# Seven block products in the last down projection: 28 of its 44 input tiles, between the up tiles that follow

## The chip, the cores and the metric

The kernel runs on one core of one Trainium2 chip. The metric is device time in microseconds (us), from the start to the end of one execution, lower is better; the median of several executions is compared. Five engines work side by side, each through its own instruction queue in order: PE (TensorE, matrix products), DVE (VectorE) and ACT (ScalarE) for elementwise work, POOL, and SP, which here only starts the transfers of weights from HBM. A matrix product on PE multiplies a stationary 128x128 operand with a moving operand of up to 512 columns and adds the result to a bank of PSUM.

## The reference

Two encoder layers over 272 tokens (16 learned ones and 256 of the input), 2048 wide, in float32. What matters here is the second half of each layer, the feed-forward part:

```python
h2 = _rmsnorm(h_stream, norm_ffn[i])
up = h2 @ w_up[i]                                     # 2048 -> 2 x 5632
u_gate = _dwconv3_centred(up[..., :D_FF], w_conv[i], b_conv[i])
u_val = up[..., D_FF:]
h_stream = h_stream + (jax.nn.silu(u_gate) * u_val) @ w_down[i]   # 5632 -> 2048
```

The first half of a layer (projections, attention, a Fourier branch, gates, output projection) is not touched. After the last layer the 16 learned tokens are dropped, so the last down projection is needed for 256 tokens only.

## The kernel before

Activations lie transposed, channels on the 128 partitions and tokens along the free dimension; 128 channels are a tile. The down projection has 44 input tiles and 16 output tiles.

**Precision.** A float32 product is made of three cheaper ones: each operand is split into a high part (rounded to the type fp32r) and a low part (the rest), and high x high, high x low and low x high are added in PSUM. Weights are the stationary operand, activations the moving one.

**Weight chunks.** All weights come as one long list of chunks (`chunks`, L152) of 128 partitions x 1024 float32, 512 KB each: four input tiles by two output tiles. SP loads a chunk into one of 4 buffers `raw` (L161), ACT rounds it into `wh` (L202), DVE subtracts into `wl` (L205). `wh` and `wl` have 3 buffers each. So the cast of chunk i+3 cannot begin before PE has finished with chunk i, and the load of chunk i+4 not before DVE has finished with chunk i.

**Groups.** `group` (L229) takes the chunks of one pair of output tiles and issues their matmuls. Where 2 x 256 columns fit a bank (the last layer, L923), high and low activations lie side by side and one matmul of 512 columns (L253) does high x high and high x low, and one of 256 (L254) does low x high; otherwise there are three (L257 to L259). After every second step of the group, `step` runs a piece of the work in `shadow` (generators pushed by other stages) and `pump` a pending split.

**Feed-forward.** For a pass of input tiles (`FF_SPLIT`, 24 and then 20 tiles), a loop over pairs of tiles runs the gate half of the up projection (group `ug`, four chunks, 258 or 272 columns) and the value half (`uv`, four chunks). DVE and ACT make the convolution, the silu and the product in between (L946 to L967) and leave its high and low part in `gHL`. Then eight groups `d` of the down projection go over all tiles of the pass, and DVE adds each to the residual stream `XT` (L976, L982) or, in the last pass of the last layer, to `ot`, which ACT's queue sends out (L979, L980).

**Order.** The Python code emits the instructions of each engine, and a scheduler behind it may move an instruction within its engine's queue where its operands allow it. The order that comes out is fixed in the program.

Of the kernel before, what the change touches and what calls it, by code (L numbers as in the profile page):

```python
# [10 lines left out]
F32 = mybir.dt.float32  # L11
# [23 lines left out]
FF_SPLIT = (24, 20)  # L35
# [10 lines left out]
)  # L46
HC = 64
# [69 lines left out]
def encoder_kernel(ctx, tc, xT, params, consts, bmat, w_in, w_abr, w_four, w_f64, w_out, w_up, w_down, outT):  # L117
    nc = tc.nc
    per = ctx.enter_context(tc.tile_pool(name="per", bufs=1))
# [6 lines left out]
    for l in range(DEPTH):  # L126
        def g(w, mg, k0, k1):
            return [(w[l, mg, c], CW) for c in range(k0 // CW, k1 // CW)]
# [16 lines left out]
        for c, n in enumerate(FF_SPLIT):  # L145
            for i in range(k0 // MG, (k0 + n) // MG):
                order.append(((l, "ug", i), g(w_up, i, 0, KT)))
                order.append(((l, "uv", i), g(w_up, FT // MG + i, 0, KT)))
            for mg in range(8):
                order.append(((l, "d", c, mg), g(w_down, mg, k0, k0 + n)))  # L150
# [3 lines left out]
    wl_at = [WL_AT.get(k[:2], 0) for k, chs in order for _ in chs]  # L154
# [54 lines left out]
    shadow = []  # L209

    def push(gen, wait=0):
        shadow.append([wait, gen])

    def step(force=False):
        for s in shadow:
            s[0] -= 1
        for s in list(shadow):
            if force or s[0] <= 0:
                try:
                    s[0] = next(s[1])  # L220
                except StopIteration:
                    shadow.remove(s)
                return

    def drain():
        while shadow:
            step(True)

    def group(key, rhs, width, tag="mm"):  # L229
# [5 lines left out]
        nk = CW * len(chs)  # L235
        for j in range(len(chs)):
# [4 lines left out]
            st["next"] += 1  # L241
            cm = [(c, m) for c in range(CW) for m in range(MG)]
            if j == len(chs) - 1:
                cm.sort(key=lambda v: v[1])
# [227 lines left out]
    for l in range(DEPTH):  # L472
# [447 lines left out]
        with tc.tile_pool(name=f"ffn{l}", bufs=1) as fp:  # L920
            hold = {}
            push(norm_stats(hold), 8)
            fused = 2 * W2 <= 512  # L923
# [10 lines left out]
            for c, n in enumerate(FF_SPLIT):  # L934
                gHL = fp.tile([P, FF_SPLIT[0], 2, XP], F32R, tag="gHL", name="gHL")
                gH, gL = (gHL[:, :, e, G_AT[l][e]:G_AT[l][e] + T] for e in range(2))
                for i in range(k0 // MG, (k0 + n) // MG):
                    ps = group((l, "ug", i), xr(lo), W)
                    drain()
# [16 lines left out]
                    for m in range(MG):  # L956
                        j = 2 * i + m - k0
                        cv = cs[m]
                        val = ps[m][:, :W2]
                        if fused:  # L960
                            v = fp.tile([P, W2], F32, tag="v", name="v", bufs=2)
                            nc.scalar.copy(v, ps[m][:, W2:2 * W2])
                            nc.vector.tensor_tensor(v, v, val, op=ALU.add)
                            val = v
                        nc.vector.tensor_tensor(cv[:, lo2:T], cv[:, lo2:T], val, op=ALU.mult)
                        nc.scalar.copy(gH[:, j, lo2:T], cv[:, lo2:T])
                        nc.vector.tensor_tensor(gL[:, j, lo2:T], cv[:, lo2:T], gH[:, j, lo2:T].bitcast(F32), op=ALU.subtract)  # L967
                lastc = c == len(FF_SPLIT) - 1
                for mg in range(8):
                    two = fused and not (lastc and mg == 7)  # L970
                    ps = group((l, "d", c, mg), (lambda kt: (both(gHL, kt, G_AT[l]),)) if two
                               else (lambda kt: (gH[:, kt, lo2:T], gL[:, kt, lo2:T])), W2)
# [12 lines left out]
                k0 += n  # L985
# [51 lines left out]
```

## Time and profile before

| | before |
|---|---|
| median of 3 runs | 2530.57 us (2529.23 to 2531.3) |
| profiled execution | 2531.57 us |
| span of its instructions | 2529.6 us |
| PE busy | 2519.5 us, granted clock at full speed throughout |
| DVE busy / ACT busy | 1688.4 us / 1210.1 us |
| read from HBM / written | 457.35 MB / 2.10 MB |

"Busy" is the time in which an engine had at least one instruction under way; matmuls overlap one another, so their single durations add up to more than the time they take, and the price of one matmul is read from the distance between two starts. The feed-forward part of layer 0 begins at about 524 us and that of the last layer at about 1797.5 us. The last one has four stages: 12 pairs of up groups to 2064, the first down pass to 2194.5, 10 pairs of up groups to 2417, the second down pass to the end.

### The profile page before, as it was taken

The numbers are of one execution on the slowest core, as the hardware profiler recorded it, in microseconds if no ns is written. First come the engines' busy times: TensorE is split into PE (matmuls) and PEld (weight loads), VectorE is DVE, ScalarE is ACT, GpSimd is POOL, SyncE is SP. The second block draws the span as 40 slices with busy tenths as digits, with TensorE's granted clock in tenths as the row PEclk, the third lists the DMA queues.
The fourth block names the chain that finished last, engine by engine and source line by source line (L and its number), as shares of the span: only waits on it lengthen the run. The fifth ranks groups of instructions, "written<-read, shape, count | busy, mean of one in ns | idle before, by whom it ended". The sixth has DMA issues, their size and how long they took to land.

```text
span 2529.6 us, 47876 instructions
## 1 busy us (share of the span) xinstructions
PE 2519.5 (100%) x19740; PEld 2461.2 (97%) x19740; DVE 1688.4 (67%) x2691; ACT 1210.1 (48%) x1741; POOL 18.3 (1%) x37
## 2 busy tenths in 40 slices
PE   9999999999999999999999999999999999999999
PEld 9999999999999999999999999999999998999988
DVE  7687866766665446566566877677766665566654
ACT  6455544554444334444444554445545543454543
POOL 0000000000000000000000000000000000000000
PEclk9999999999999999999999999999999999999999
DMA  6444555555555555555554545555555555555564
GB/s 239 164 158 160 195 184 190 189 177 181 179 182 178 181 180 179 182 178 180 180 174 153 178 159 195 197 198 194 189 191 189 189 190 194 195 187 191 191 204 163
DMA packets 132155, 465.34 MB, mean 184 GB/s; under 512 B 15328, under 2 KB 19296, under 8 KB 131936
## 3 DMA queue, kind: packets, MB, share of 16 engines
q1 hardware_dynamic: 127568, 457.37, 53.2%
q10 hardware_dynamic: 4368, 4.92, 0.6%
q8 instruction: 154, 2.52, 0.4%
q14 instruction: 65, 0.53, 0.1%
HBM read 457.35 MB, written 2.10 MB: 182 GB/s over the span
## 4 chain that ended last, share of the span: by engine, by line
PE 96%; DVE 2%; ACT 1%; DMA 1%; issue 0%; ACTq 0%; SPq 0%; DVEq 0%
PE ps_ug L257 7%; PE ps_ug L259 7%; PE ps_ug L258 7%; PE ps_uv L253 6%; PE ps_d L253 6%; PE ps_d L259 4%; PE ps_d L257 4%; PE ps_d L258 4%; PE ps_uv L259 3%; PE ps_uv L257 3%; PE ps_uv L258 3%; PE ps_uv L254 3%; PE ps_d L254 3%; PE ps_o L257 2%; PE ps_o L259 2%; PE ps_o L258 2%
## 5 line engine op out<-in xcount | busy, mean ns | idle before, releaser
L205 DVE TENSOR_TENSOR wl<-raw,wh 128x1024 fp32r<-128x1024 f32 (+1 forms) x835 | 1016.8, 1220 | 672.8 <-ACT wh L202 669.4
L202 ACT CAST wh<-raw 128x1024 fp32r<-128x1024 f32 (+1 forms) x834 | 870.3, 1046 | 960.5 <-PE ps_ug L258 159.4
L257 PE MATMUL ps_ug<-xHL,wh 128*128 128x272 f32 (+1 forms) x1408 | 398.0, 283 | 0.0
L259 PE MATMUL ps_ug<-xHL,wl 128*128 128x272 f32 (+1 forms) x1408 | 396.5, 282 | 0.0
L258 PE MATMUL ps_ug<-xHL,wh 128*128 128x272 f32 (+1 forms) x1408 | 395.7, 281 | 0.0
L257 PEld LDWEIGHTS ps_ug<-xHL,wh 128*128 128x128 f32 x1408 | 264.3, 188 | 0.9
L258 PEld LDWEIGHTS ps_ug<-xHL,wh 128*128 128x128 f32 x1408 | 264.5, 188 | 0.1
L259 PEld LDWEIGHTS ps_ug<-xHL,wl 128*128 128x128 f32 x1408 | 264.3, 188 | 0.0
L253 PE MATMUL ps_uv<-xHL,wh 128*128 128x512 f32 x704 | 245.1, 391 | 0.0
L253 PE MATMUL ps_d<-gHL,wh 128*128 128x512 f32 x664 | 225.9, 389 | 0.0
L257 PE MATMUL ps_d<-gHL,wh 128*128 128x272 f32 (+1 forms) x744 | 212.5, 286 | 0.0
L259 PE MATMUL ps_d<-gHL,wl 128*128 128x272 f32 (+1 forms) x744 | 211.9, 285 | 0.0
L258 PE MATMUL ps_d<-gHL,wh 128*128 128x272 f32 (+1 forms) x744 | 211.2, 284 | 0.0
L257 PE MATMUL ps_uv<-xHL,wh 128*128 128x272 f32 x704 | 201.3, 286 | 0.0
L259 PE MATMUL ps_uv<-xHL,wl 128*128 128x272 f32 x704 | 200.6, 285 | 0.0
L258 PE MATMUL ps_uv<-xHL,wh 128*128 128x272 f32 x704 | 199.9, 284 | 0.0
L254 PE MATMUL ps_uv<-xHL,wl 128*128 128x256 f32 x704 | 198.4, 282 | 0.0
L254 PE MATMUL ps_d<-gHL,wl 128*128 128x256 f32 x664 | 183.3, 276 | 0.0
L253 PEld LDWEIGHTS ps_uv<-xHL,wh 128*128 128x128 f32 x704 | 131.9, 187 | 27.2
L253 PEld LDWEIGHTS ps_d<-gHL,wh 128*128 128x128 f32 x664 | 124.6, 188 | 25.5
L257 PE MATMUL ps_ga<-xHL,wh 128*128 128x272 f32 (+1 forms) x512 | 147.0, 287 | 0.1
L257 PE MATMUL ps_gf<-xHL,wh 128*128 128x272 f32 (+1 forms) x512 | 145.9, 285 | 0.1
(286 smaller groups left out, 5862.1 us busy)
## 6 DMA issues: line engine op xcount, KB each, us to landing
raw<-in_w_up SPq DMA_DIRECT2D x352, 512.0 KB, 3.5
raw<-in_w_in SPq DMA_DIRECT2D x206, 512.0 KB, 3.6
raw<-in_w_down SPq DMA_DIRECT2D x176, 512.0 KB, 3.5
raw<-in_w_out SPq DMA_DIRECT2D x64, 512.0 KB, 3.8
raw<-in_w_four SPq DMA_DIRECT2D x32, 512.0 KB, 4.1
raw<-in_w_abr SPq DMA_DIRECT2D x32, 512.0 KB, 3.6
qs<-qp ACTq DMA_DIRECT2D x32, 68.0 KB, 3.8
outT<-ot ACTq DMA_DIRECT2D x16, 128.0 KB, 3.6
```

The costliest lines, as they stand in the source:

```text
L202: nc.scalar.copy(h[:, a:b], r[:, a:b])
L205: nc.vector.tensor_tensor(lo[:, a:b], r[:, a:b], h[:, a:b].bitcast(F32), op=ALU.subtract)
L253: nc.tensor.matmul(o2, h[:, c, sl], ab, start=kt == 0, stop=False)
L254: nc.tensor.matmul(o, lo[:, c, sl], ab[:, 0, :], start=False, stop=kt == nk - 1)
L257: nc.tensor.matmul(o, h[:, c, sl], a, start=kt == 0, stop=False)
L258: nc.tensor.matmul(o, h[:, c, sl], b, start=False, stop=False)
L259: nc.tensor.matmul(o, lo[:, c, sl], a, start=False, stop=kt == nk - 1)
```

## The change

**Passes.** In the last layer the input tiles are taken in three passes of 14, 14 and 16 instead of 24 and 20 (layer 0 keeps its two). Only the third pass runs eight groups `d`. The 28 tiles of the first two passes are multiplied otherwise.

**Seven products.** Two input tiles and two halves of the 256 tokens make a 2x2 block matrix A (of 128x128 blocks), and the rows of the down weights for these two tiles, cut into two halves of 1024 output columns, a 2x2 block matrix B. Eight block products would give the 2x2 result; here seven products of sums and differences of blocks are made, in the order and with the destinations of `PRODUCTS`. Here the activations are the stationary operand (a 128x128 block) and the weights the moving one: a block of B is one chunk of 128 x 1024, and its product takes six matmuls of 512 columns (two column halves by three precision terms). A product is accumulated over the 7 tile pairs of a pass in two PSUM banks and then added to one to four quarters of `C4` (`gather`; for the first product ACT copies instead).

**Weights.** Three of the seven weight operands are blocks as they are (a copy `w_blk` of these rows, laid out by the host), four are sums or differences. `weight_sums` makes those while layer 0's feed-forward part runs: for each of 14 tile pairs ACT's queue loads four blocks, DVE makes four subtractions of 128 x 1024, and ACT's queue stores four results in HBM (`tsum`).

**Placement.** The 49 block chunks of a pass are mixed evenly into the list of chunks of the next pass's up groups, which makes 49 between 56 chunks in the second pass and 49 between 64 in the third. They go through `raw`, `wh` and `wl` like the others. `combos` makes the activation blocks, their sums and their high and low parts on ACT and DVE, out of float32 activations (`g0`, `g1`: the high and low split of `gHL` is not made in these passes).

**Back.** `C4` has tokens on the partitions, so `turned` transposes it on PE in 32 blocks of 128x128 during the first `d` group and DVE adds the result to `XT`.

```diff
-FF_SPLIT = (24, 20)
+FF_SPLIT = ((24, 20), (14, 14, 16))
+NPR = sum(FF_SPLIT[-1][:2]) // 2
+PRODUCTS = ((1, "11 12 21 22"), (2, "11"), (6, "12 21 22"), (7, "21 22"), (4, "21"), (5, "12 22"), (3, "12"))
...
+    tsum = [[dram.tile([P, D // 2], F32, name=f"ts{q}_{e}") for e in range(4)] for q in range(NPR)]
...
+                for p, _ in PRODUCTS:
+                    for q in range(FF_SPLIT[l][c - 1] // 2):
+                        src = {1: w_blk[2 * (q0 + q), 0], 2: w_blk[2 * (q0 + q) + 1, 0], 3: w_blk[2 * (q0 + q) + 1, 1],
+                               5: tsum[q0 + q][0], 7: tsum[q0 + q][1], 6: tsum[q0 + q][2], 4: tsum[q0 + q][3]}[p]
+                        xs_.append((src.rearrange("p (c m) -> p c m", c=CW), (c - 1, p, q)))
...
+                        mixed.append(ch)
+                        at += 1
+                        while done < len(xs_) and done * slots < at * len(xs_):
+                            mixed.append(xs_[done])
+                            done += 1
...
+            def weight_sums():
+                tt = nc.vector.tensor_tensor
+                for q in range(NPR):
+                    b = [fp.tile([P, D // 2], F32, tag=f"b{e}", name=f"b{e}") for e in range(4)]
+                    for e in range(4):
+                        nc.scalar.dma_start(b[e], w_blk[2 * q + e // 2, e % 2])
+                        yield 3
+                    yield 12
+                    tt(b[0], b[1], b[0], op=ALU.subtract)
+                    yield 4
+                    tt(b[1], b[3], b[1], op=ALU.subtract)
...
+                    for e, k in enumerate((0, 1, 3, 2)):
+                        nc.scalar.dma_start(tsum[q][e], b[k])
+                        yield 3
...
+            def combos(c):
...
+                        if p in (1, 2, 4):
+                            x = A[{1: "11", 2: "12", 4: "22"}[p]]
+                        else:
+                            x = fp.tile([P, 4, P], F32, tag="sx", name="sx", bufs=2)[:, :m]
...
+                        cb = fp.tile([P, 2, 4, P], F32R, tag="cb", name="cb", bufs=3)
+                        nc.scalar.copy(cb[:, 0, :m], x)
+                        tt(cb[:, 1, :m], x, cb[:, 0, :m].bitcast(F32), op=ALU.subtract)
...
+            def gather(c, p, ps):
+                for to in dict(PRODUCTS)[p].split():
+                    at = 2 * int(to[0]) + int(to[1]) - 3
+                    for e in range(2):
+                        o = C4[:, at, 512 * e:512 * e + 512]
+                        if c == 0 and p == 1:
+                            nc.scalar.copy(o, ps[e])
+                        else:
+                            nc.vector.tensor_tensor(o, o, ps[e], op=ALU.add)
+                        yield 2
...
+                for e in range(2):
+                    wh, wl = (t_.rearrange("p c m -> p (c m)")[:, 512 * e:512 * e + 512] for t_ in (h, lo))
+                    for a, (s_, w) in enumerate(((0, wh), (0, wl), (1, wh))):
+                        nc.tensor.matmul(ps[e], cb[:, s_, q - q4], w, start=q == 0 and a == 0, stop=q == n - 1 and a == 2)
...
+            def turned():
+                for mt in range(0, KT, 2):
+                    pt = psum.tile([P, 512], F32, tag="aux", name="ps_ct")
+                    for m in range(2):
+                        for hh in range(2):
+                            src = C4[:, 2 * hh + (mt + m) // 8, (mt + m) % 8 * P:(mt + m) % 8 * P + P]
+                            nc.tensor.transpose(pt[:, P * (2 * m + hh):P * (2 * m + hh) + P], src, ident)
+                    x = XT[:, mt:mt + 2, NM:T]
+                    nc.vector.tensor_tensor(x, x, pt.rearrange("p (m t) -> p m t", m=2), op=ALU.add)
```

**The order that comes out, at three places.** First DVE, in the last layer's up groups, where the value group of tile pair 10 ends. `wlN` is the split of chunk N, `v` and `cv` are the two steps behind the value group `ps_1_uv_10`. Before:

```order
L205 TENSOR_TENSOR wl689_24478<-raw689_24357,wh689_24477 128x1024
L963 TENSOR_TENSOR v_24493<-v_24493,ps_1_uv_10_0_24403 128x256
L965 TENSOR_TENSOR cv_24389<-cv_24389,v_24493 128x256
L205 TENSOR_TENSOR wl690_24516<-raw690_24405,wh690_24515 128x1024
L967 TENSOR_TENSOR gHL_21844<-cv_24389,gHL_21844 128x256
L963 TENSOR_TENSOR v_24499<-v_24499,ps_1_uv_10_1_24404 128x256
L965 TENSOR_TENSOR cv_24397<-cv_24397,v_24499 128x256
L205 TENSOR_TENSOR wl691_24546<-raw691_24427,wh691_24545 128x1024
L967 TENSOR_TENSOR gHL_21844<-cv_24397,gHL_21844 128x256
L205 TENSOR_TENSOR wl692_24576<-raw692_24449,wh692_24575 128x1024
L205 TENSOR_TENSOR wl693_24606<-raw693_24471,wh693_24605 128x1024
```

Between two splits stand at most three short rows of 256 columns. The same place now (with the changed kernel's line and chunk numbers; `cb` and `sx` are activation blocks and their sums, `g0` and `g1` the float32 activations of the first and second pass):

```order
L233 TENSOR_TENSOR wl717_25107<-raw717_25029,wh717_25106 128x1024
L1128 TENSOR_TENSOR v_25122<-v_25122,ps_1_uv_10_0_24990 128x256
L1024 TENSOR_TENSOR cb_25336<-sx_25326,cb_25336 128x512
L1131 TENSOR_TENSOR g1_23801<-cv_24976,v_25122 128x256
L1014 TENSOR_TENSOR sx_25658<-g0_22128 128x512
L1128 TENSOR_TENSOR v_25126<-v_25126,ps_1_uv_10_1_24991 128x256
L233 TENSOR_TENSOR wl718_25141<-raw718_25051,wh718_25140 128x1024
L1131 TENSOR_TENSOR g1_23801<-cv_24984,v_25126 128x256
L1017 TENSOR_TENSOR sx_25658<-sx_25658,g0_22128 128x512
L233 TENSOR_TENSOR wl719_25170<-raw719_25063,wh719_25169 128x1024
L1020 TENSOR_TENSOR sx_25658<-g0_22128,sx_25658 128x512
L233 TENSOR_TENSOR wl720_25185<-raw720_25085,wh720_25184 128x1024
```

The splits and the rows of the value group are still there, without the two of `gHL`; between them now stand four rows of 512 columns for activation blocks, and before the next split (721) three more rows of 512 columns, not shown, that add a product to `C4`.

Second PE, just behind that place, where a block chunk (717) stands between two chunks of gate group 11:

```order
L303 MATMUL ps_1_ug_11_1_25131<-xHL_125,wh716_25090 128x258
L304 MATMUL ps_1_ug_11_1_25131<-xHL_125,wh716_25090 128x258
L305 MATMUL ps_1_ug_11_1_25131<-xHL_125,wl716_25091 128x258
L1052 MATMUL ps_x040_25164<-wh717_25106,cb_24998 128x512
L1052 MATMUL ps_x040_25164<-wl717_25107,cb_24998 128x512
L1052 MATMUL ps_x040_25164<-wh717_25106,cb_24998 128x512
L1052 MATMUL ps_x041_25165<-wh717_25106,cb_24998 128x512
L1052 MATMUL ps_x041_25165<-wl717_25107,cb_24998 128x512
L1052 MATMUL ps_x041_25165<-wh717_25106,cb_24998 128x512
L303 MATMUL ps_1_ug_11_0_25130<-xHL_125,wh718_25140 128x258
L304 MATMUL ps_1_ug_11_0_25130<-xHL_125,wh718_25140 128x258
L305 MATMUL ps_1_ug_11_0_25130<-xHL_125,wl718_25141 128x258
```

Six matmuls of 512 columns have moved in between the 24 of one up chunk and the 24 of the next; before, the next up chunk followed at once.

Third ACT, early in layer 0's feed-forward part, where `weight_sums` runs (`b` are its four blocks, `ts` its results in HBM):

```order
L975 DMA b3_7845<-in_w_blk 128x1024
L230 CAST wh181_7164<-raw181_7028 128x1024
L987 DMA ts1_0_61<-b0_7842 128x1024
L1113 ACTIVATE cv_7188<-u_7186,prm_126 128x272
L1113 ACTIVATE cv_7196<-u_7194,prm_126 128x272
L230 CAST wh182_7212<-raw182_7066 128x1024
L987 DMA ts1_1_62<-b1_7843 128x1024
L1117 ACTIVATE cv_7188<-cv_7188 128x272
L1117 ACTIVATE cv_7196<-cv_7196 128x272
L230 CAST wh183_7242<-raw183_7096 128x1024
```

The casts and the activations are those of before; the loads and stores of `weight_sums` have moved in between, and a store stands behind the DVE row that makes its block.

More of the change, by code (lines that the diff above doesn't have):

```diff
@@ L46 @@
 )
+GN = FF_SPLIT[-1][2] * 2 * SEQ + 64
+G_LAST = 0
 HC = 64
@@ L214, in step @@
     def step(force=False):
+        for s in list(behindhand):
+            s[0] -= 1
+            if s[0] <= 0:
+                try:
+                    s[0] = next(s[1])
+                except StopIteration:
+                    behindhand.remove(s)
         for s in shadow:
```

145 lines of the change are left out of this document (124 added, 21 removed).

## The prediction

> **What bounds the kernel now.** I read the page first: busy time by engine, and the chain that ended last.
>
> ```profile
> PE 2519.5 (100%) x19740; PEld 2461.2 (97%) x19740; DVE 1688.4 (67%) x2691; ACT 1210.1 (48%) x1741; POOL 18.3 (1%) x37
> PE 96%; DVE 2%; ACT 1%; DMA 1%; issue 0%; ACTq 0%; SPq 0%; DVEq 0%
> ```
>
> PE is busy all the time and makes 96% of the chain. Busy may hide waits, so I read next who waited for whom, for PE and for its weight loads (microseconds in total, times, longest).
>
> ```profile
> PE ps_f L314 <- ACT wh L202: 3.0, 4, 1.2
> PE ps_s L293 <- DVE wl L205: 1.9, 3, 0.9
> ...
> PEld ps_s L293 <- DVE wl L205: 2.5, 3, 1.1
> ```
>
> All waits of the span are a few microseconds, none in the feed-forward parts. The second row matters below: the 16 `s` groups of the Fourier branch are the only place where chunks are short for PE, and there a split comes late three times, by 1.1 us at most. Then the stages of the last feed-forward part (first up groups, first down pass, second up groups), a piece of layer 0's, and nine microseconds of layer 0's query groups:
>
> ```profile
> core 0: us, PE busy (x) PEld busy (x) DVE busy (x) ACT busy (x) POOL busy (x), PEclk, DMA share, GB/s
> 1797.50:2064.00 266.50, 266.50 (x1917) 251.11 (x1917) 182.12 (x270) 137.70 (x193) 0.85 (x1) 1.00 0.56 190
> 2064.00:2194.50 130.50, 130.50 (x769) 115.83 (x768) 70.99 (x83) 51.46 (x51) 0.00 (x0) 1.00 0.57 194
> 2194.50:2417.00 222.50, 222.50 (x1604) 209.70 (x1603) 150.60 (x219) 112.90 (x157) 0.00 (x0) 1.00 0.55 190
> ...
> 524.00:790.00 266.00, 266.00 (x2177) 265.92 (x2176) 165.94 (x235) 124.79 (x163) 0.85 (x1) 1.00 0.52 179
> ...
> 104.00:113.00 9.00, 9.00 (x76) 9.00 (x75) 5.43 (x9) 3.09 (x5) 0.00 (x0) 1.00 0.70 221
> ```
>
> PE is full at the full clock in each; DVE stands at 150.60 of 222.50, 68%, in the second up groups. So the time is the sum of PE's matmuls, and a change is worth what it takes from that sum, as long as the splits keep up.
>
> **Removed from PE.** The down projection of the 28 tiles: 28 x 16 = 448 pairs of an input and an output tile. A fused pair costs the distance from one L253 to the next; here the first and the last of 28:
>
> ```profile
> 2499.95 0.39 PE L253 MATMUL ps_d<-gHL,wh 128*128 128x512 f32 x1
> 2500.18 0.28 PE L254 MATMUL ps_d<-gHL,wl 128*128 128x256 f32 x1
> ...
> 2509.13 0.39 PE L253 MATMUL ps_d<-gHL,wh 128*128 128x512 f32 x1
> ...
> 2523.38 0.28 PE L259 MATMUL ps_d<-gHL,wl 128*128 128x256 f32 x1
> ...
> 2526.20 0.28 PE L259 MATMUL ps_d<-gHL,wl 128*128 128x256 f32 x1
> ```
>
> That is 9.18 / 27 = 0.340 us; the first down pass agrees (130.5 us for 24 x 16 pairs). In the last group, unfused, 24 steps of 256 columns take 2.82 us, 0.1175 each. The last group has 16 instead of 20 tiles, so 440 fused pairs and 8 triples go: 440 x 0.340 + 8 x 3 x 0.1175 = 149.6 + 2.8 = 152.4 us.
>
> **Added to PE.** 2 passes x 7 products x 7 pairs x 6 = 588 matmuls of 512 columns. No row shows a run of these. By the rows, such a matmul costs at most the 0.230 us from an L253 to its L254, and at least 0.340 - 0.1175 = 0.2225; by columns it is 0.340 x 512/768 = 0.2267, which I take, since it lies between the two: 133.3 us (130.8 to 135.2). [...]
>
> The transposes of `turned` are eight times four. Four of the same size in a query group:
>
> ```profile
> 105.86 0.60 PE L640 MATMUL ps_ss<-cst,qps 128*128 128x128 f32 x4
> 106.22 0.37 PE L257 MATMUL ps_q<-xHL,wh 128*128 128x272 f32 x1
> 106.43 0.29 PE L258 MATMUL ps_q<-xHL,wh 128*128 128x272 f32 x1
> 106.55 0.28 PE L259 MATMUL ps_q<-xHL,wl 128*128 128x272 f32 x1
> ```
>
> 0.36 us, and the matmul behind takes 0.21 instead of 0.12: 0.45 us, eight times 3.6. PE alone: -152.4 + 133.3 + 3.6 = **-15.5 us** (-18.0 to -13.6).
>
> **Do the splits keep up?** Costs of the rows that prepare a chunk, and of a DVE row of 512 columns (mean ns after the busy time):
>
> ```profile
> L205 DVE TENSOR_TENSOR wl<-raw,wh 128x1024 fp32r<-128x1024 f32 x830 | 1013.9, 1224 | 672.5 <-ACT wh L202 669.1
> L202 ACT CAST wh<-raw 128x1024 fp32r<-128x1024 f32 x830 | 868.1, 1048 | 960.2 <-PE ps_ug L258 159.4 <-PE ps_d L258 140.0 <-PE ps_d L253 131.6
> ...
> L190 DVE TENSOR_TENSOR wpm<-raw 128x512 f32<-128x512 f32 x64 | 42.0, 687 | 18.4 <-DMA raw<-in_w_four 17.8
> ```
>
> A block chunk keeps PE for 6 x 0.2267 = 1.36 us, an up chunk for 222.5 / 80 = 2.78 us, and both need one split. Second pass: PE 0.7 x 222.5 + 49 x 1.36 = 222.4 us. DVE 0.7 x 150.6 = 105.4, plus 49 x 1.224 = 60.0, plus for the activation blocks 14 rows of 512 (0.687) and 14 of 384 (some 0.55, between 256 and 512) = 17.3, plus 20 gathers at 0.687 = 13.7: 196 us, 88%. Third pass: PE 178.0 + 66.6 = 244.6, DVE 120.5 + 60.0 + 17.3 + 28 x 0.687 = 217, 89%. ACT comes to about 65%. On the average both keep up; what counts is how late one split may be. Around a chunk boundary of PE (2294.72):
>
> ```profile
> 2294.72 0.39 PE L253 MATMUL ps_uv<-xHL,wh 128*128 128x512 f32 x1
> ```
> ```profile
> 2292.08 1.05 ACT L202 CAST wh<-raw 128x1024 fp32r<-128x1024 f32 x1 [1.73 <-PE ps_ug L258]
> ```
> ```profile
> 2293.16 1.22 DVE L205 TENSOR_TENSOR wl<-raw,wh 128x1024 fp32r<-128x1024 f32 x1 [1.55 <-ACT wh L202]
> ...
> 2298.72 1.22 DVE L205 TENSOR_TENSOR wl<-raw,wh 128x1024 fp32r<-128x1024 f32 x1
> 2299.85 0.42 DVE L953 TENSOR_TENSOR cv<-cv,rstdB 128x256 f32<-128x256 f32 x1
> ```
>
> The boundary before was at 2294.72 - 2.78 = 2291.94; the cast of the chunk three further on starts 0.14 us later, its split 1.08 after that and ends 1.22 later: ready 2.45 us after PE let go of a buffer. PE wants it two chunks on: so far after 5.55 us, with a block among the two after 4.14. The slack falls from 3.1 to 1.7 us, and DVE's other rows must fit into it; a split holds DVE for 1.13 us until the next row.
>
> I went through the place that the order shows, with t = 0 at the end of the last up chunk of value group 10 (715), rows in order, each at its price. Split 718 is ready at 3.3 (PE wants it at 4.1), 719 at 5.4 (6.9), 720 at 7.1 (8.3), 721, behind three gathers, at 10.1 (11.1). Behind a gate group the tightest split is ready 0.5 us before PE wants it. So by the rows no split is late, but by margins of 0.5 to 1 us. The nearest row that shows such a place is the 16 `s` groups with 2.5 us of waits; for 14 products with their group ends I take the same, **+2.5 us**. The ends: nothing (a gain is excluded, PE does not wait there now) and 1.1 us, the longest wait, at each of the 14 + 16 group ends of both passes, 33 us.
>
> Loads: 105 chunks of 0.524 MB in 222.4 us are 248 GB/s against 190 now; by the windows' 0.55 share that is 0.72 of the queues. SP loads chunk i+4 when the split of chunk i is done; four chunks last 8.3 us, less 2.45 leaves 5.8 us for a landing of 3.5:
>
> ```profile
> raw<-in_w_up SPq DMA_DIRECT2D x352, 512.0 KB, 3.5
> ```
>
> Hidden; a split that is over 2 us late would make the load late too.
>
> **Layer 0.** `weight_sums` puts 56 subtractions (1.224 us: 68.5 us) on DVE, at 62% there, and 112 transfers on ACT's queue, at 47%, over some 650 us (14 pairs, about 16 chunks each, a chunk 24 matmuls at the 0.12 us above, 2.9 us). What waits: a subtraction for its blocks to land, a split behind it; a store for the subtraction, a cast behind it; PE for these. A transfer keeps ACT for 2.44 / 4 = 0.61 us:
>
> ```profile
> 106.18 2.44 ACTq L646 DMA_DIRECT2D qs<-qp  x4
> 108.74 2.00 ACT L202 CAST wh<-raw 128x1024 fp32r<-128x1024 f32 x2 [4.34 <-issue]
> ```
>
> There ACT casts nothing for 4.34 us, and PE is busy 9.00 of 9.00 us (the last window above). Chunks of layer 0 leave 2 x 2.9 - 2.45 = 3.4 us of slack, so I take **+0.5 us**; the ends are nothing and one longest wait per pair, 14 x 1.1 = 15 us. Without that cover, DVE's 68.5 us or ACT's 112 x 0.61 = 68 us would stand on the path.
>
> **The end.** DVE's eight adds behind the transposes (5.5 us) and four splits fit into the first down group (10.9 + 3.6 us). The 14 x 2 activations less to split and the 32 adds less to `XT` are off the path. Nothing else is nearer the end than before.
>
> **Sum:** -15.5 + 2.5 + 0.5 = -12.5 us. The profiled execution took 2531.57 us (span 2529.6 and 1.97 around it) and would take 2519.1; its time is 1.0 above the median, so the median goes from 2530.57 to **2518 us**, between 2513 and 2526 if the reading is right.
>
> **Rivals.** *Late splits at the group ends* (slower): DVE at 88 to 89% serves short chunks with a slack of 1.7 us, and each of the 30 group ends makes PE wait. It decides from 15.5 / 30 = 0.52 us each; with 0.7, between the two longest waits of the rows and half of them, it is 21 us and the time 2530.6 - 15.5 + 21 + 0.5 = 2537 us. For it: the margins of 0.5 us and the late splits in the `s` groups. Against it: those came only three times in 16 groups. *The sums of layer 0 cost what the products gain*: at one late split of 1.1 us per pair, 15 us, the time is 2532; against it stands the gap of 4.34 us that PE did not feel. *The blocks are cheaper and nothing waits*: at 0.2225 per matmul and no wait it is -18.0, 2513 us. [...]
>
> **How the numbers follow.** Under 2525.5 is faster and over 2535.6 slower by 0.2%, about what a measurement of this kernel tells from no change. Forecast 0.56 (0.52 faster, 0.04 same), cheaper blocks 0.12 (faster), sums of layer 0 0.12 (0.03, 0.07, 0.02), late splits 0.20 (0.04 same, 0.16 slower). Together 0.67 faster, 0.15 same, 0.18 slower. The range reaches from below the cheap blocks, 2511, to the late splits, 2537; the forecast's own range is 2513 to 2526.
>
> **What would show it.** The distance between two starts inside a block chunk should be 0.223 to 0.230 us. In the list of waits, PE behind `wl` in the up groups should stay at a few microseconds in all; tens of them, after gate and value groups of the last layer, are the late splits. The second and third pass should take about 222 and 245 us, with DVE near 85 to 89%, and the last layer's up groups should begin at 1797.5 us as before. The forecast is wrong if PE idles more than 15 us in the two passes, or if the stretch before the last layer grows by more than a few microseconds.

## The result, and the profile after

The changed kernel takes **2549.35 us** (median of 4 runs, 2546.66 to 2550.88) where the kernel before takes 2530.12 us in the same comparison (4 runs): a ratio of 1.0075, 95% interval 1.0057 to 1.0092. It is slower by 0.75%. The forecast was 2518 us, faster, with a range of 2511 to 2537 us; the time lies outside it and on the other side.

The profiled execution took 2548.31 us, its span is 2546.4 us (before: 2531.57 and 2529.6 us). First the page, with busy times, TensorE's granted clock and the chain that ended last:

```profile
PE 2518.7 (99%) x19456; PEld 2447.9 (96%) x19456; DVE 1830.7 (72%) x2841; ACT 1258.4 (49%) x1791; POOL 19.2 (1%) x37
...
PE   9999999999998999999999999999999999999999
...
DMA  6545656689998755555554545666555787777765
GB/s 238 171 150 167 194 184 192 184 290 359 339 361 321 258 180 182 176 181 182 179 178 158 171 158 184 198 198 200 188 190 190 233 244 244 247 242 237 241 221 167
...
PE 89%; DMA 5%; DVE 4%; issue 1%; ACT 1%; ACTq 0%; SPq 0%; DVEq 0%
```

PE has 284 instructions fewer (19740 before) and yet the same busy time to a microsecond (2519.5), and the span is 17 us longer: what was saved has been filled up again, and idle time has come on top. The chain shows where to look: DMA and DVE have 9% of it where they had 3%. The dip in PE (13th slice, 64 us each) falls where DMA moves 320 to 360 GB/s, which is layer 0's feed-forward part, where the sums run.

The largest single number is a start time. The last layer's first gate matmul starts at 1796.5 us before and at 1822.3 us now, and layer 0's first at 523.8 and 522.6 us. So the stretch between them grew from 1272.7 to 1299.7 us: **27.0 us are lost before the last layer's feed-forward part begins**. From there to the end of the span it is 2529.6 - 1796.5 = 733.1 us before and 2546.4 - 1822.3 = 724.1 us now: **9.0 us are gained where the products are.** The windows of both parts, layer 0 first (columns as in the prediction):

```profile
524.00:600.00 76.00, 72.67 (x583) 71.56 (x582) 57.59 (x81) 34.69 (x47) 1.76 (x1) 1.00 0.90 331
600.00:700.00 100.00, 92.06 (x730) 91.21 (x730) 74.16 (x94) 40.76 (x53) 0.00 (x0) 0.97 0.93 349
700.00:800.00 100.00, 97.55 (x779) 97.12 (x778) 75.25 (x98) 43.18 (x56) 0.00 (x0) 0.98 0.94 345
800.00:900.00 100.00, 95.53 (x775) 94.79 (x774) 57.69 (x65) 38.12 (x42) 0.00 (x0) 1.00 0.77 270
900.00:1000.00 100.00, 100.00 (x820) 100.00 (x819) 50.56 (x57) 38.10 (x40) 0.00 (x0) 1.00 0.55 180
```

```profile
1822.30:1978.40 156.10, 156.10 (x1125) 147.13 (x1124) 104.97 (x152) 78.66 (x104) 0.85 (x1) 1.00 0.59 189
1978.40:2204.00 225.60, 225.60 (x1416) 203.41 (x1415) 182.94 (x238) 134.94 (x169) 0.00 (x0) 1.00 0.78 243
2204.00:2452.00 248.00, 248.00 (x1578) 224.61 (x1577) 205.87 (x278) 146.22 (x188) 0.00 (x0) 1.00 0.76 240
2452.00:2544.50 92.50, 91.36 (x578) 82.31 (x576) 54.81 (x75) 32.45 (x33) 0.00 (x0) 1.00 0.58 180
```

From 524 to 900 us PE is not full, and from 600 to 800 its granted clock is under 1; by 900 all is as before. Up to 800 us DMA stands at 0.90 to 0.94 of its queues where it had 0.52. In the last layer's two passes with blocks PE is full at the full clock.

Who waited, in layer 0's feed-forward part (us in total, times, longest): PE, then DVE, each from its own list.

```profile
PE ps_uv L305 <- DVE wl L233: 16.8, 10, 4.8
PE ps_ug L305 <- DVE wl L233: 1.2, 1, 1.2
```
```profile
DVE b L978 <- DMA b<-in_w_blk: 29.4, 9, 5.9
DVE b L980 <- DMA b<-in_w_blk: 19.5, 10, 4.4
```

None of these rows was there before. DVE stood 48.9 us in front of subtractions whose blocks had not landed, and PE stood 18.0 us in front of splits that DVE had not made. Each of PE's 11 waits ends at most 8 us after such a wait of DVE, and none of the 11 late splits waited for its cast: each starts right behind the DVE row before it. One such place in the timeline (start, duration, then the idle time before it and what ended it), of DVE and of PE:

```profile
686.19 0.50 DVE L1115 SCALAR_TENSOR_TENSOR cv<-u,prm,cv 128x271 f32<-128x271 f32 x1
692.60 1.22 DVE L978 TENSOR_TENSOR b<-b,b 128x1024 f32<-128x1024 f32 x1 [5.91 <-DMA b<-in_w_blk]
693.75 0.43 DVE L1118 TENSOR_TENSOR cv<-cv,rstdB 128x272 f32<-128x272 f32 x1
694.10 0.49 DVE L1116 SCALAR_TENSOR_TENSOR cv<-u,prm,cv 128x271 f32<-128x271 f32 x1
694.51 2.35 DVE L233 TENSOR_TENSOR wl<-raw,wh 128x1024 fp32r<-128x1024 f32 x2
```
```profile
690.55 0.29 PE L303 MATMUL ps_uv<-xHL,wh 128*128 128x272 f32 x1
690.68 0.28 PE L304 MATMUL ps_uv<-xHL,wh 128*128 128x272 f32 x1
695.78 0.60 PE L305 MATMUL ps_uv<-xHL,wl 128*128 128x272 f32 x1 [4.82 <-DVE wl L233]
696.18 0.43 PE L303 MATMUL ps_uv<-xHL,wh 128*128 128x272 f32 x1
696.40 0.43 PE L304 MATMUL ps_uv<-xHL,wh 128*128 128x272 f32 x1
```

DVE takes its rows in order. At 686.7 its next row is a subtraction, the block lands at 692.6, and two splits that could have been made long before (their casts ended at 686.9 and 688.9) come only at 694.51. PE runs out of splits at 690.9 and stands for 4.82 us. Then it pays again: its matmuls are 0.227 us apart until about 700.9, where 0.12 is usual.

### The profile page after: what moved, and what is told of

It is laid out like the page before. It is cut to its first block, busy times and chain, and to the rows that moved or that the text cites. A ratio compares the mean times of both kernels' runs of the same rounds, so it can differ in the third digit from the quotient of the medians.

```text
span 2546.4 us, 47886 instructions
## 1 busy us (share of the span) xinstructions
PE 2518.7 (99%) x19456; PEld 2447.9 (96%) x19456; DVE 1830.7 (72%) x2841; ACT 1258.4 (49%) x1791; POOL 19.2 (1%) x37
## 4 chain that ended last, share of the span: by engine, by line
PE 89%; DMA 5%; DVE 4%; issue 1%; ACT 1%; ACTq 0%; SPq 0%; DVEq 0%
PE ps_uv L299 6%; PE ps_ug L303 5%; PE ps_x L1052 5%; PE ps_ug L304 5%; PE ps_ug L305 5%; PE ps_d L305 4%; PE ps_d L303 4%; PE ps_d L304 4%; PE ps_uv L300 3%; DMA b<-in_w_blk 3%; PE ps_o L303 2%; PE ps_uv L305 2%; PE ps_o L305 2%; PE ps_o L304 2%; PE ps_gf L303 2%; PE ps_ga L303 2%
## 5 line engine op out<-in xcount | busy, mean ns | idle before, releaser
L233 DVE TENSOR_TENSOR wl<-raw,wh 128x1024 fp32r<-128x1024 f32 (+1 forms) x877 | 1065.1, 1219 | 487.1 <-ACT wh L230 483.7
L230 ACT CAST wh<-raw 128x1024 fp32r<-128x1024 f32 (+1 forms) x876 | 913.6, 1046 | 896.9 <-PE ps_ug L304 176.6
L305 PEld LDWEIGHTS ps_uv<-xHL,wl 128*128 128x128 f32 x704 | 133.9, 190 | 19.7 <-DVE wl L233 19.7
L303 PE MATMUL ps_o<-mH,wh 128*128 128x272 f32 (+1 forms) x512 | 144.6, 283 | 0.0
L305 PE MATMUL ps_ga<-xHL,wl 128*128 128x272 f32 (+1 forms) x512 | 144.5, 282 | 0.0
```

What stands on the lines that cost most here:

```text
L230: nc.scalar.copy(h[:, a:b], r[:, a:b])
L233: nc.vector.tensor_tensor(lo[:, a:b], r[:, a:b], h[:, a:b].bitcast(F32), op=ALU.subtract)
L303: nc.tensor.matmul(o, h[:, c, sl], a, start=kt == 0, stop=False)
L305: nc.tensor.matmul(o, lo[:, c, sl], a, start=False, stop=kt == nk - 1)
```

## The experiments

Twelve kernels, compared by their times and, since the loss lies in one place, by the distance between the first gate matmuls of the two layers ("the distance", 1272.7 us before, 1299.7 after; the runs without a loss below lie between 1271.6 and 1273.5).

**1. The sums taken out.** The seven products stay; the four parked weights of each pair are replaced by plain quarters of `w_blk`.

```diff
-                               5: tsum[q0 + q][0], 7: tsum[q0 + q][1], 6: tsum[q0 + q][2], 4: tsum[q0 + q][3]}[p]
+                               5: w_blk[2 * (q0 + q), 1], 7: w_blk[2 * (q0 + q), 0], 6: w_blk[2 * (q0 + q) + 1, 1], 4: w_blk[2 * (q0 + q) + 1, 0]}[p]
...
-                behindhand.append([60, weight_sums()])
```

> The pair sums of layer 0 are left out, and the products read plain quarters of w_blk in place of the parked differences, so the output isn't the reference's; all products, their loads and all of the last layer stay. Theory A (the loss of 25.8 us lies in layer 0, made by the sums, and the last layer gains 9.0): 2548 - 26 = 2522 (2519 to 2526), the last layer's first up matmul at 1796 to 1798 as before, the part from there to the end 724 as in the changed kernel. Rival B (the products delay the stream, or layer 0 is late for another reason, such as the order of the code): over 2540. If A is right, no matmul of layer 0 waits behind a split.

2521.19 us (5 runs; ratio 0.9967, 0.9954 to 0.9980). The distance is 1273.5 us, no matmul of layer 0's feed-forward part waits behind a split, and from the last layer's first gate matmul to the end it is 2520.6 - 1796.5 = 724.1 us, as in the changed kernel. Theory A holds.

**2. The sums alone,** put into the kernel before; nothing reads what they store.

```diff
+            if l == DEPTH - 2:
+                behindhand.append([60, weight_sums()])
```

> The kernel before, with nothing but the sums added to layer 0's FFN (loads, four subtractions a pair, stores into the parked tiles, which nothing reads). Theory A: 2530 + 26 = 2556 (2550 to 2560), all of it between the start of layer 0's FFN at 524 and the last layer's first up matmul. Rival B: 2530 to 2534.

2557.33 us (4 runs; ratio 1.0110, 1.0095 to 1.0125), the distance 1300.1 us. The two runs together: the sums cost some 27 us and the products gain 9 us, and they add up.

**3. The sums paced.** The order that runs is made by a scheduler that moves a row ahead in its queue when its operands and its buffer allow. That is what happened to the sums: the code gives a pair 64 steps, which are 16 chunks. The first subtractions of 14 pairs ran from 532.6 to 836.2 us, one pair in 23.4 us. Between the first subtractions of two pairs DVE made 6 to 9 splits, 7.2 on the average (94 in 13 distances), not 16. Here each row of the sums is tied to its place behind the last split that was issued before it on the same engine.

```diff
-            nc.scalar.copy(h[:, a:b], r[:, a:b])
+            st["act"] = nc.scalar.copy(h[:, a:b], r[:, a:b]).ins
...
-                    s[0] = next(s[1])
+                    with tc.issue_after(st["act"]), tc.issue_after(st["dve"]):
+                        s[0] = next(s[1])
```

> The changed kernel whole, only that each instruction of the sums keeps its place in its engine's queue behind the split that stood last when the code issued it, so that a pair takes some 16 chunks (about 45 us) where it took 22.7 us. Theory A1 (the loss comes from the pace: DMA at 345 GB/s and transfers that land late): the last layer's first up matmul is at 1796 to 1801, the run takes 2522 to 2527, DMA share in layer 0's FFN 0.70 to 0.80 in place of 0.90 to 0.94, faster than the kernel before by 0.2 to 0.4 per cent. Rival A2 (the sums cost what they cost by their number, 56 subtractions and 112 transfers, at any pace): 2540 to 2549.

2521.61 us (7 runs; ratio 0.9968, 0.9957 to 0.9980): the whole change, and faster than the kernel before. The distance is 1272.3 us. A pair takes 46.9 us, with 16 splits (first subtractions at 584.9 to 1194.0 us). The windows of this kernel:

```profile
600.00:700.00 100.00, 100.00 (x821) 100.00 (x820) 69.55 (x94) 46.41 (x61) 0.00 (x0) 1.00 0.79 276
700.00:800.00 100.00, 100.00 (x820) 100.00 (x820) 70.47 (x96) 46.80 (x62) 0.00 (x0) 1.00 0.78 266
```

PE is full, with the same 56 subtractions and 112 transfers. A2, a price by their number, falls; against the run without sums they cost 0.4 us here, which is less than the runs differ among themselves. What the pace did it by is still open: it thins the transfers, and it moves each subtraction away from its loads.

**4. The transfers without the subtractions,** at the changed kernel's pace; the parked tiles hold plain quarters.

```diff
-                    tt(b[0], b[1], b[0], op=ALU.subtract)
...
-                    tt(b[2], b[2], b[3], op=ALU.subtract)
-                    yield 4
+                    yield 16
```

> The changed kernel with the 56 subtractions left out: the loads and stores stand at the same places of ScalarE's queue, and the parked tiles hold plain quarters, so the output isn't the reference's. Theory D (crowded DMA queues hold up the stream's own tiles): the loss stays, 15 us or more of 25.8, 2538 to 2549, and SyncE's raw tiles land in over 4 us. Theory V (VectorE's in-order queue stands behind a subtraction whose tile hasn't landed, and the split behind it is late): under 5 us of the loss stay, 2522 to 2527, though the DMA share is as high as before at some 345 GB/s.

2521.88 us (6 runs; ratio 0.9969, 0.9957 to 0.9981), the distance 1272.9 us. Its windows and, in the stretch from 524 to 850 us, the landing of the stream's tiles (last column, us):

```profile
600.00:700.00 100.00, 100.00 (x821) 100.00 (x820) 59.72 (x83) 45.79 (x58) 0.00 (x0) 1.00 1.00 380
700.00:800.00 100.00, 100.00 (x821) 100.00 (x820) 62.88 (x89) 47.63 (x61) 0.00 (x0) 1.00 1.00 380
```
```profile
raw<-in_w_up SPq DMA_DIRECT2D x91, 512.0 KB, 6.7
```

The queues are fuller than in the changed kernel and the stream's tiles land in 6.7 us (3.5 in the kernel before, 6.4 in the changed one), and PE does not feel it. Crowded queues alone cost nothing here: 0.7 us more than run 1, within the spread of the runs (D falls).

**5. The subtractions without the transfers,** four to each 8 chunks (23.5 us a pair), on tiles that are loaded once, with the rows tied to their places as in run 3.

```diff
+                b = [fp.tile([P, D // 2], F32, tag=f"b{e}", name=f"b{e}") for e in range(4)]
+                for e in range(4):
+                    nc.scalar.dma_start(b[e], w_blk[e // 2, e % 2])
+                yield 14
                 for q in range(NPR):
...
                     tt(b[2], b[2], b[3], op=ALU.subtract)
-                    yield 4
-                    for e, k in enumerate((0, 1, 3, 2)):
-                        nc.scalar.dma_start(tsum[q][e], b[k])
+                    yield 26
```

> Only the 56 subtractions stay of layer 0's sums, four to each 8 chunks as they ran in the changed kernel; their tiles are loaded once, nothing is stored, and the products read plain quarters, so the output isn't the reference's. Theory V (not the work of the subtractions but VectorE's standing still in front of a tile that hasn't landed makes the splits late): 2520 to 2525, VectorE as busy between 524 and 800 as in the changed kernel, no matmul behind a split. Rival W (the subtractions' own time, bunched, makes the splits late): 2535 to 2549.

2521.44 us (one run), the distance 1273.0 us. DVE is busier than in the changed kernel and PE is full:

```profile
600.00:700.00 100.00, 100.00 (x820) 100.00 (x819) 80.06 (x101) 46.16 (x59) 0.00 (x0) 1.00 0.57 179
700.00:800.00 100.00, 100.00 (x821) 100.00 (x820) 80.59 (x107) 47.46 (x62) 0.00 (x0) 1.00 0.56 177
```

W falls at this pace, a little slower in chunks than the changed kernel's 7.2: DVE has room for the subtractions. So neither part costs anything by itself, and the theories that blame one of them alone are out. What is left is V, the standing in front of a tile that hasn't landed, and the load of both parts together. The next two kernels vary the distance between a load and its subtraction, though not it alone: the steps between the transfers change as well.

**6. Fast, but the subtractions far behind their loads.** 8 chunks a pair (24.5 us), near the 7.2 of the changed kernel; the rows are kept in place as in run 3, and 12 steps or more lie between a load and the first subtraction.

```diff
-                    for e in range(4):
+                    for e in (0, 1, 3, 2):
                         nc.scalar.dma_start(b[e], w_blk[2 * q + e // 2, e % 2])
-                        yield 3
-                    yield 12
+                        yield 1
+                    yield 11
...
```

> The changed kernel whole, a pair of sums to each 8 chunks as it ran there (22.7 us), but each kept at its place, with the first subtraction 14 steps, some 3.5 chunks or 10 us, behind the load of its first operand's last tile or before. Theory V (it is VectorE's standing in front of a tile that hasn't landed): the loss falls from 25.8 us to under 6, 2522 to 2528, at a DMA share of 0.85 or more between 600 and 800, and what is left comes with waits of the subtractions for their loads. Rival A1 (the pace is the cause): 2535 to 2549.

2534.16 us (8 runs; ratio 1.0015, 1.0005 to 1.0025), the distance 1285.9 us: 13 us of the 27 are left. No subtraction waits for its load any more. What waits is ScalarE for the stream's own tiles, 20 times (in the changed kernel 8 times, 14.6 us; before, no row of this kind):

```profile
ACT wh L230 <- DMA raw<-in_w_up: 38.2, 20, 4.5
```

Both theories miss: V said under 6 us of loss; A1 said 2535 us or more, which the time misses by 0.8 us, but half of the loss is won at an almost unchanged pace.

**7. Slow, but the subtractions right behind their loads.** 16 chunks a pair; the four loads of a pair now go out together.

```diff
-                        yield 3
-                    yield 12
+                    yield 1
                     tt(b[0], b[1], b[0], op=ALU.subtract)
...
-                    yield 12
+                    yield 35
```

> The paced kernel's 16 chunks a pair, but the first subtraction of a pair stands right behind its loads. Theory V: VectorE stands still in front of the first two subtractions of each pair for some 4 to 7 us, the splits behind them are late, and 1 to 2 us of each of 14 pairs reach TensorE: 2535 to 2550, though the DMA share is under 0.80. Rival A1 (the pace is the cause): 2521 to 2525.

2532.56 us (8 runs, 2529.72 to 2539.56; ratio 1.0016, 1.0005 to 1.0026); the distance in the profiled run is 1281.0 us, 8 us lost. DVE's list:

```profile
DVE b L978 <- DMA b<-in_w_blk: 26.4, 14, 4.8
...
DVE b L980 <- DMA b<-in_w_blk: 6.4, 13, 1.4
```

27 waits, two in nearly every pair, at a DMA share of 0.76. Each of PE's 7 waits is for a split with such a subtraction one to three rows in front of it. The mechanism of V works at the slow pace too, where A1 expected nothing, but at 8 us in the profile and 11 in the median it is smaller than V's 13 to 28.

**8. As run 6, the transfers spread** over 6 steps in place of 3.

```diff
                         nc.scalar.dma_start(b[e], w_blk[2 * q + e // 2, e % 2])
-                        yield 1
-                    yield 11
+                        yield 2
+                    yield 7
...
                         nc.scalar.dma_start(tsum[q][e], b[k])
-                        yield 1
-                    yield 6
+                        yield 2
+                    yield 2
```

> As e9_fast_far (whole change, 8 chunks a pair, subtractions far behind their loads), but a pair's four loads and four stores are spread over 6 steps each in place of 3. In e9 no subtraction waited for a load, and 12 to 13 us of loss were left, with ScalarE waiting 38 us for late raw tiles. Theory Q (the bunches of transfers in front of the raw tiles make them late): the loss falls under 6 us, 2522 to 2527, ScalarE waiting under 15 us for raw tiles. Rival R (transfers at 340 GB/s together with the subtractions' work on VectorE leave the splits no margin, bunched or not): 2530 to 2536, ScalarE's wait as long.

2529.50 us (8 runs; ratio 0.9999, 0.9987 to 1.0010), the distance 1280.3 us: 8 us of loss are left. ScalarE's wait for raw tiles is longer still, and PE's is short but not gone:

```profile
ACT wh L230 <- DMA raw<-in_w_up: 51.8, 27, 3.1
```
```profile
PE ps_uv L306 <- DVE wl L233: 5.1, 8, 1.4
```

Spreading wins 5 of the 13 us, as part of Q had it, but not by fewer or shorter waits in sum; with 17.9 us for the down projection's tiles ScalarE waits 69.7 us in all, and only the longest wait falls, from 4.5 to 3.5 us. The rest goes with R, though the time lies 0.5 us under its range: transfers at 346 GB/s with the subtractions between the splits leave a loss even where none of them stands in front of its own load, while transfers at 380 GB/s without subtractions leave none (run 4).

PE's 8 waits and the longer step behind each make 7.3 of the 8 us, and all have one form. One of them, on ACT, DVE and PE:

```profile
628.81 1.05 ACT L230 CAST wh<-raw 128x1024 fp32r<-128x1024 f32 x1 [3.05 <-DMA raw<-in_w_up]
```
```profile
629.89 1.23 DVE L233 TENSOR_TENSOR wl<-raw,wh 128x1024 fp32r<-128x1024 f32 x1 [1.74 <-ACT wh L230]
...
636.37 1.22 DVE L233 TENSOR_TENSOR wl<-raw,wh 128x1024 fp32r<-128x1024 f32 x1
```
```profile
637.64 0.52 PE L306 MATMUL ps_uv<-xHL,wl 128*128 128x272 f32 x2 [1.37 <-DVE wl L233]
```

A cast waits for a late tile, the split behind it comes late, and then eight rows of DVE, three of them subtractions, stand before the next split, 6.48 us from start to start (in run 5 at most 4.92). Nine pairs have these rows. In seven of them ScalarE had waited 5.6 to 6.7 us for tiles in the 12 us before, and PE waits 0.24 to 1.37 us; of the other two, one (5.0 us) has no wait of PE and one (4.6 us) has 0.28. Whether three subtractions in a bunch would cost something without late tiles, no run shows.

**9 to 11. The price of a block.** The other miss of the prediction is small: 9 us gained where 13 were forecast. A block chunk takes 6 x 0.231 us (mean over 97 blocks of the start of the chunk behind minus the start of the block, divided by 6), and the gate chunk behind a block takes 2.846 us (39 chunks) where one took 2.77 to 2.78. Two runs move the low split of the block chunks within its tile (0, 16 and 48 words), one leaves out the blocks' loads and splits and lets each multiply with the splits of the chunk before.

```diff
-    wl_at = [0 if ch[1] != CW else WL_AT.get(k[:2], 0) for k, chs in order for ch in chs]
+    wl_at = [16 if ch[1] != CW else WL_AT.get(k[:2], 0) for k, chs in order for ch in chs]
```

> The paced kernel, with the low split of the block chunks 16 words further into its tile. Theory O (the place of the streamed operand sets the price of a block matmul): 0.223 to 0.228 us from one block matmul to the next in place of 0.232, some 588 x 0.004 = 2.4 us off, 2519. Rival P (0.232 whatever the place): distances and time unchanged within 1 us.

> As the run before, with 48 words in place of 16. Theory O: another distance than at 0 and at 16 words, between 0.222 and 0.24 us. Rival P: 0.232 again.

```diff
         src, n = chunks[i]
+        if n != CW:
+            return
...
-            h, lo = splits.pop(i)
+            if tag_ == CW:
+                h, lo = splits.pop(i)
```

> The paced kernel without the 98 loads and splits of the block tiles: each block multiplies with the splits of the chunk before it, so the output isn't the reference's; every matmul stays. Theory N (the splits that VectorE and ScalarE write while TensorE streams slow the block matmuls and the chunk after a block): blocks at 0.223 to 0.228 us, an up chunk after a block at 2.77 like the others, the two passes with blocks at 221 to 223 and 243 to 245 us in place of 225.6 and 248, 2515 to 2517. Rival P (the price is that of the form, 128x512 streamed from a weight tile): blocks at 0.232 still, passes at most 1.5 us shorter each.

| run | block matmul, us apart | gate chunk behind a block, us | first block to the end of the last, us | time, us |
|---|---|---|---|---|
| 0 words (run 3) | 0.2312 | 2.846 | 467.7 | 2521.6 (7 runs) |
| 16 words | 0.2325 | 2.823 | 466.8 | 2519.7 (1) |
| 48 words | 0.2312 | 2.794 | 465.2 | 2519.2 (1) |
| no loads and splits of blocks | 0.2316 | 2.829 | 467.5 | 2524.3 (1) |

The block's price stays at 0.2312 to 0.2325 us at each of the three places of the operand, and also without the blocks' own loads and splits (0.2316): P holds for the price of a block, O and N fall. What the place changes is the chunk behind the block, which no theory had, P with its unchanged time neither: 0.05 us for each of the gate chunks between 0 and 48 words. (The last run's time says little here: it reached layer 0's feed-forward part at 525.3 us, 3.3 us after run 3, and its distance is 1273.4 us.)

**12. The paced kernel with 48 words, again.**

> The paced kernel with 48 words in place of 0 for the blocks' low split, as one look had it: 2519 to 2520, 0.4 per cent faster than the kernel before, and 2 us below the paced kernel's 2521.6. Rival: 2521 to 2522, the one look's 2519.2 having been a draw.

**2518.98 us** (5 runs, 2518.46 to 2519.69; ratio 0.9955, 0.9942 to 0.9969), 2.6 us under run 3, each set against the kernel before at 2530.1 us. From the last layer's first gate matmul to the end it takes 721.6 us, as in the single run with 48 words, where run 3 takes 724.1: the rival, a draw, falls. Of the versions run it is the fastest.

## Why the prediction was wrong

**Removed work: right.** The prediction had 152.4 us less and 3.6 us of transposes, together -148.8 us. The two down passes took 130.5 + (2529.6 - 2417.0) = 243.1 us before; now the one with the transposes takes 2546.4 - 2452.0 = 94.4 us: -148.7 us.

**Added matmuls: right in kind, 2.6 us short.** The term was 588 x 0.2267 = 133.3 us, with 135.2 as its upper bound; it measured 588 x 0.2312 = 135.9 us, just outside. The rows of a block (start, duration; the fourth row holds two):

```profile
1981.47 0.28 PE L305 MATMUL ps_ug<-xHL,wl 128*128 128x258 f32 x1
1981.59 0.39 PE L1052 MATMUL ps_x<-wh,cb 128*128 128x512 f32 x1
1981.82 0.40 PE L1052 MATMUL ps_x<-wl,cb 128*128 128x512 f32 x1
1982.06 0.62 PE L1052 MATMUL ps_x<-wh,cb 128*128 128x512 f32 x2
1982.52 0.39 PE L1052 MATMUL ps_x<-wl,cb 128*128 128x512 f32 x1
1982.75 0.40 PE L1052 MATMUL ps_x<-wh,cb 128*128 128x512 f32 x1
1982.98 0.28 PE L303 MATMUL ps_ug<-xHL,wh 128*128 128x258 f32 x1
```

The distance within a fused pair, 0.230 us, was the better row than the split by columns. The bound itself came from two starts that are given to 0.01 us.

**The neighbours: missed.** The prediction kept the up chunks at their old price. The two passes took 225.6 + 248.0 = 473.6 us; less 135.9 for the blocks, 337.7 us remain for 120 up chunks, 2.81 us each, where the passes before had 2.78 (333.8 us). That is 3.9 us, and the runs with 48 words show that 2.5 of them hang on where the block's split lies.

**Late splits in the last layer: right that they don't decide, 2.5 us too dear.** No matmul of the up groups waited behind a split there. DVE stood at 81 and 83% in the two passes (182.9 of 225.6, 205.9 of 248.0) where 88 and 89 were forecast. So the rival with waits at the group ends fell, and the margins of 0.5 us that I walked through held. The passes came out at 225.6 and 248.0 us for 222.4 and 244.6, by the two terms above and not by waits. In all, 2.6 and 3.9 us were left out and 2.5 us were put in that did not come, so this part gained 9.0 us where 13.0 were forecast; that the miss is 4 us and not 6.5 is luck.

**Layer 0's sums: the step that failed.** The prediction wrote "over some 650 us (14 pairs, about 16 chunks each)" and took +0.5 us, at most 15. The 16 chunks were counted from the code's steps. The order of the changed kernel had the pairs at less than half that distance: from the first subtraction of one pair to that of the next it has 19 to 26 rows of DVE, with 7.2 splits among them on the average, and the 14 pairs took some 330 us. I read that order, a piece of which stands in the part on the change, for what lies between two casts and not for how far apart two pairs are. Three things rested on the 650 us. The load on DMA would have been near the 0.78 of the paced run; it was 0.90 to 0.94. The only landing time in the prediction was 3.5 us; the loads of the sums took this long (page, last column):

```profile
b<-in_w_blk ACTq DMA_DIRECT2D x56, 512.0 KB, 7.0
ts<-b ACTq DMA_DIRECT2D x56, 512.0 KB, 5.2
```

And the longest wait per pair was taken from rows in which DVE never waits for a transfer, 1.1 us; DVE's longest wait was 5.9 us, above the 3.4 us of slack that I had worked out for layer 0. The prediction named this very queueing ("a subtraction for its blocks to land, a split behind it") and then priced it from a row in which only ScalarE paused. The other queueing it named, a cast behind a store that waits for a subtraction, came too (ScalarE waited 22.1 us in 7 such places), but no late split stood behind such a cast. The sign that the prediction had named for being wrong, a longer stretch before the last layer, came with 27.0 us. With the pace as I assumed it, run 3 gives 2521.6 us: 3.6 us from the forecast, inside its own range, and on the forecast's side; but the pace alone does not make it, since run 7 loses 11 us at the same pace with its subtractions close behind their loads. The rival "the sums cost what the products gain" had the right mechanism and 15 us for it, where it was 27.

**What the 27 us are made of.** PE's rows show 18.0 us of idle. From start to start, less the usual 0.122 us, these waits cost 20.1 us, the matmul behind each 1.2 us in all, and two stretches at half the clock (the rows of 0.97 and 0.98) 4.0 us. Some 2 us lie in smaller delays. As to causes, the runs show: transfers alone nothing, subtractions alone nothing (8 chunks a pair), both at half the pace nothing, both at 8 chunks a pair without a wait for their loads 8 to 13 us, both with those waits 27 us, the waits at half the pace 8 us. So some 14 to 19 us go with DVE's standing in front of blocks that had not landed, a difference between runs that also differ in pace (7.2 and 8 chunks) and in the steps between transfers, and the rest with late tiles of the stream meeting a DVE that has less room to catch up. A likely link, only argued, is that SyncE may load the next raw tile only when DVE has made a split out of the old one, so that a late split delays a later load: its list has `SPq L190 <- DVE wl L233` with 11.1 us as the longest wait in the changed kernel, and 3.5 in the paced one. How much of run 6's 13 us each of these two makes is open.

## What to carry to other kernels

Work that is "spread over the kernel" is spread only as far as the order that really runs: count the distance between two of its rounds in the queues, not in the code's steps, and tie it there if the distance matters. A row that waits for a transfer on an engine that also feeds the bottleneck cost the wait and not its own duration here (5.9 us in front of a row of 1.2), and the transfer's landing has to be priced at the load that the change itself puts on the queues (7.0 us for the blocks at a share of up to 0.94, where the prediction had 3.5 from the stream's tiles at 0.52). Two additions that each hide completely cost 27 us together here, so a cover proven for one of them says little of both.

## What the runs showed of the hardware

**A late split can cost twice.** After PE's wait of 4.82 us the granted clock (third column from the end) is half, and full again from about 700.9 us, where the matmuls are 0.12 us apart once more:

```profile
690.83:695.78 4.95, 0.13 (x2) 0.00 (x0) 3.18 (x5) 1.10 (x2) 0.00 (x0) 0.83 0.24 92
695.78:699.50 3.72, 3.72 (x16) 3.72 (x17) 3.04 (x4) 0.27 (x1) 0.00 (x0) 0.50 0.94 290
699.50:704.00 4.50, 4.50 (x33) 4.50 (x32) 2.33 (x3) 1.37 (x2) 0.00 (x0) 0.84 1.03 411
```

At 0.50 for some 5.1 us, that is 2.5 us on top of 4.8. A second wait was followed by half the clock too, though it was only half as long:

```profile
771.23 0.39 PE L305 MATMUL ps_uv<-xHL,wl 128*128 128x272 f32 x1 [2.41 <-DVE wl L233]
```
```profile
772.60:776.00 3.40, 3.40 (x18) 3.40 (x17) 3.37 (x4) 0.69 (x1) 0.00 (x0) 0.50 0.90 272
```

After the wait of 2.48 us at 821 us, however, the next matmuls are 0.12 us apart as ever, so the length of the wait alone does not decide. The clock stood at half for some 5.1 us in the first place and for 3.4 us in the second; what sets it off, the runs do not show.

**A core's queues moved 380 GB/s** (run 4, two windows of 100 us at a share of 1.00) while PE kept its pace: 821 and 821 matmuls in 100 us, as in the same windows of the kernel before, at 179 to 180 GB/s.
